# The first layer's feed-forward by seven products of half blocks, on one core

## The chip, the cores and the metric

The kernel runs on one core of a Trainium2 chip. The metric is the device time of one launch in microseconds (us), as the median of some runs. Its engines have queues of their own and work side by side: TensorE (PE) multiplies matrices, VectorE (DVE) and ScalarE (ACT) work on tiles of 128 partitions, GpSimd (POOL) does little here and SyncE (SP) issues most of the transfers. An engine takes its instructions in the order in which they stand in its queue.

## What is computed

Three layers run over 512 positions of 1,024 features in float32. The first layer is a feed-forward, a mixer and a second feed-forward; the change touches the two feed-forwards alone.

```python
D_MODEL, D_FF, SEQ = 1024, 2816, 512

def swiglu(x, w_gate, w_up, w_down):
    return (jax.nn.silu(x @ w_gate) * (x @ w_up)) @ w_down

x = x + 0.5 * swiglu(rms_norm(x, norm_ffn1), ffn1_gate, ffn1_up, ffn1_down)
x = x + mixer(x)
x = x + 0.5 * swiglu(rms_norm(x, norm_ffn2), ffn2_gate, ffn2_up, ffn2_down)
```

## The kernel before

Activations lie with features on the partitions: a tile is 128 features by 512 positions. A float32 product is made of three matmuls. Each operand is split into a high part and a rest (`split`: a cast on ACT, then a subtraction on DVE), and PE adds hi x hi, hi x lo and lo x hi. So a block of 128 output features over 8 input tiles is 24 matmuls of 512 columns into one PSUM bank.

`dense` runs one such block. For it `weights` loads the block's weights (`raw`, 512 KB, on SP's queue), casts them on ACT (`whi`) and subtracts on DVE (`wlo`), from pools of two buffers; `banks` gives the number of PSUM banks for each use (d for blocks, m for small things).

`ffn_swiglu` goes through the 22 tiles of hidden features in parts of 8, 8 and 6 (`FF_TILES`). For each tile it runs a gate block and an up block; DVE multiplies each by r, ACT takes the silu, DVE multiplies both, and `split` makes the hidden tile's two parts. Behind each part come the eight down blocks, each over the part's tiles, and DVE adds half of the block to x. The features enter the first products multiplied by their gain only; r, the reciprocal root of the mean square, is a factor of each position, and is applied behind the product. Its sum of squares (`sum_sq`, on ACT and DVE) and `rstd` (a sum over partitions by matmuls with ones, small steps, two matmuls that spread the result over the partitions, a copy) are written behind the first two blocks. A scheduler puts each engine's instructions in order by priorities, which `sooner` raises (`lead` is 50 here), so that the order in the program need not be that of the code.

The mixer and the other two layers stand in the same order in both kernels.

Of the kernel before, what the change touches and what calls it, by code (L numbers as in the profile page):

```python
# [263 lines left out]
class Model:  # L264
# [336 lines left out]
    def ffn_swiglu(self, f, g):  # L601
        nc, d = self.nc, self.d
        self.lead = 50
        with ExitStack() as es:
            es.enter_context(self.banks(d=4, m=4))
            hp = self.pool(es, f + "h", 2)
            act = self.pair(self.ap, NKT, "x")
            for k in range(NKT):
                self.norm_split(act, g, k)
            j0, r = 0, None  # L610
            for part, n in enumerate(FF_TILES):
                hh = hp.tile([P, 8, S], F32R, tag="hh", name="hh")
# [1655 lines left out]
```

## Time and profile before

| | us |
|---|---|
| median of three runs | 2797.9 (2794.69 to 2798.13) |
| the profiled execution | 2792.82, span 2790.8 |
| PE, DVE, ACT busy in it | 2737.6, 1674.2, 1156.4 |
| first feed-forward | 8.40 to 372.80 |
| second feed-forward | 732.50 to 1096.10 |

The profile is one execution; its span leaves out what lies around the program, 2 us. Busy time is the sum of an engine's instructions, where matmuls overlap and are counted once.

### The profile page before, as it was taken

Reading aid. Unit: us, or ns where it says so; the run is one execution under the profiler, and the core shown is the slowest. Engines: PE = TensorE matmul, PEld = TensorE weight load, DVE = VectorE, ACT = ScalarE, POOL = GpSimd, SP = SyncE. Lnnn points to the kernel's source line nnn. Section 1 sums busy time; section 2 is a strip of 40 time slices with the busy share of each in tenths; the row PEclk is TensorE's granted clock in tenths of the full one; section 3 lists DMA queues with packets and bytes.
Section 4 is the critical chain, followed back from the end, with each engine's and each line's share of the span. In section 5 each row is a group of like instructions: output and inputs, shape, how many; then the busy total and the mean of one; then the engine's idle time right before and its main releaser. Section 6 shows DMA issues by size and latency. Waiting matters only on the chain. (4 is left out here: it accounts for less than half of the span.)

```text
span 2790.8 us, 36154 instructions
## 1 busy us (share of the span) xinstructions
PE 2737.6 (98%) x14502; PEld 2224.3 (80%) x14502; DVE 1674.2 (60%) x2699; ACT 1156.4 (41%) x1758; POOL 79.5 (3%) x165
## 2 busy tenths in 40 slices
PE   8999999999999999999999999999999999999998
PEld 6888877767788888787888888888887878888887
DVE  5444476776643447686345885546846985466456
ACT  4222354553422224565233434444457544343334
POOL 0000000000000000000000011110000000000000
PEclk9999999999999999999999999999999999999999
DMA  4333231110233333322342344443224442312232
GB/s 140 98 99 94 91 131 42 46 51 28 77 97 98 98 96 128 114 83 78 95 138 94 108 164 142 138 133 110 84 76 140 148 148 102 120 69 83 69 105 76
DMA packets 83864, 281.16 MB, mean 101 GB/s; under 512 B 10097, under 2 KB 10609, under 8 KB 82929
## 3 DMA queue, kind: packets, MB, share of 16 engines
q1 hardware_dynamic: 76464, 255.28, 28.2%
q0 software_dynamic: 5888, 18.09, 1.9%
q10 hardware_dynamic: 1344, 5.49, 0.6%
q8 instruction: 113, 1.85, 0.3%
q14 instruction: 55, 0.44, 0.0%
HBM read 254.44 MB, written 23.07 MB: 99 GB/s over the span
## 5 line engine op out<-in xcount | busy, mean ns | idle before, releaser
L366 ACT CAST whi<-raw 128x1024 fp32r<-128x1024 f32 (+4 forms) x454 | 450.5, 993 | 1207.8 <-PE ps_d L391 809.9
L390 PE MATMUL ps_d<-xhi,whi 128*128 128x512 f32 x1896 | 752.2, 397 | 13.9 <-ACT whi L366 9.3
L392 PE MATMUL ps_d<-xhi,wlo 128*128 128x512 f32 x1896 | 743.0, 392 | 3.5 <-DVE wlo L367 3.4
L391 PE MATMUL ps_d<-xlo,whi 128*128 128x512 f32 x1896 | 743.0, 392 | 0.0
L367 DVE TENSOR_TENSOR wlo<-raw,whi 128x1024 fp32r<-128x1024 f32 (+4 forms) x454 | 521.2, 1148 | 156.1 <-ACT whi L366 154.6
L390 PEld LDWEIGHTS ps_d<-xhi,whi 128*128 128x128 f32 x1896 | 357.0, 188 | 94.5 <-ACT whi L366 10.2
L392 PEld LDWEIGHTS ps_d<-xhi,wlo 128*128 128x128 f32 x1896 | 356.9, 188 | 80.9 <-DVE wlo L367 5.3
L391 PEld LDWEIGHTS ps_d<-xlo,whi 128*128 128x128 f32 x1896 | 357.1, 188 | 77.6 <-issue 5.0
L390 PE MATMUL ps_d<-hh,whi 128*128 128x512 f32 x608 | 237.2, 391 | 0.4 <-ACT hh L404 0.4
L392 PE MATMUL ps_d<-hh,wlo 128*128 128x512 f32 x608 | 236.8, 390 | 0.5 <-DVE wlo L367 0.5
L391 PE MATMUL ps_d<-hl,whi 128*128 128x512 f32 x608 | 237.0, 390 | 0.2 <-DVE hl L405 0.2
L390 PEld LDWEIGHTS ps_d<-hh,whi 128*128 128x128 f32 x608 | 114.1, 188 | 25.1 <-ACT hh L404 0.8
L392 PEld LDWEIGHTS ps_d<-hh,wlo 128*128 128x128 f32 x608 | 114.1, 188 | 24.9 <-DVE wlo L367 1.4
L391 PEld LDWEIGHTS ps_d<-hl,whi 128*128 128x128 f32 x608 | 114.1, 188 | 24.4 <-DVE hl L405 1.1
L625 DVE TENSOR_TENSOR hb<-ps_d,rstd 128x512 f32<-128x512 f32 x44 | 30.4, 691 | 135.9 <-PE ps_d L392 135.9
L632 DVE SCALAR_TENSOR_TENSOR x<-ps_d,x 128x512 f32<-128x512 f32 x48 | 33.2, 691 | 116.3 <-PE ps_d L392 116.2
L390 PE MATMUL ps_d<-mixhi,whi 128*128 128x512 f32 x224 | 88.8, 396 | 0.7 <-DVE x L1681 0.6
L624 DVE TENSOR_TENSOR ha<-ps_d,rstd 128x512 f32<-128x512 f32 x44 | 30.4, 691 | 95.8 <-PE ps_d L392 93.2
L392 PE MATMUL ps_d<-mixhi,wlo 128*128 128x512 f32 x224 | 87.7, 392 | 0.0
L391 PE MATMUL ps_d<-mixlo,whi 128*128 128x512 f32 x224 | 87.5, 391 | 0.0
L469 DVE TENSOR_TENSOR acc<-acc,sq 128x512 f32<-128x512 f32 x67 | 46.0, 686 | 25.7 <-ACT sq L468 25.1
L1480 DVE TENSOR_TENSOR x<-ps_d,x 128x512 f32<-128x512 f32 x32 | 22.0, 688 | 61.3 <-PE ps_d L392 61.3
(691 smaller groups left out, 4071.8 us busy)
## 6 DMA issues: line engine op xcount, KB each, us to landing
raw<-in_ffn_gu_dram SPq DMA_DIRECT2D x88, 512.0 KB, 3.5
raw<-in_w_in_dram SPq DMA_DIRECT2D x64, 512.0 KB, 3.5
raw<-in_ffn_dn_dram SPq DMA_DIRECT2D x32, 512.0 KB, 3.5
raw<-in_w_up_dram SPq DMA_DIRECT2D x32, 512.0 KB, 3.5
raw<-in_w_down_dram SPq DMA_DIRECT2D x32, 512.0 KB, 3.9
raw<-in_ret_in_dram SPq DMA_DIRECT2D x32, 512.0 KB, 3.2
raw<-in_ab_in_dram SPq DMA_DIRECT2D x28, 512.0 KB, 3.2
raw<-in_ret_v_dram SPq DMA_DIRECT2D x16, 512.0 KB, 3.2
```

Source lines behind the costliest of these rows:

```text
L366: nc.scalar.copy(hi[:, :n], raw[:, :n])
L367: nc.vector.tensor_sub(lo[:, :n], raw[:, :n], hi[:, :n].bitcast(F32))
L390: PE.matmul(ps, lhsT=hi[:, w], rhs=ah, start=first, stop=False)
L391: PE.matmul(ps, lhsT=hi[:, w], rhs=al, start=False, stop=False)
L392: PE.matmul(ps, lhsT=lo[:, w], rhs=ah, start=False, stop=last)
L469: nc.vector.tensor_add(acc, acc, sq)
L624: nc.vector.tensor_mul(a, pg, r)
L625: nc.vector.tensor_mul(b, pu, r)
L632: nc.vector.scalar_tensor_tensor(out=xm, in0=po, scalar=0.5, in1=xm, op0=ALU.mult, op1=ALU.add)
L1480: nc.vector.tensor_add(xm, po, xm)
```

## The change

In both feed-forwards of the first layer only the first 4 of the 22 tiles of hidden features keep plain blocks of 512 columns (8 blocks). The remaining 18, as gate and up 36 blocks, are taken in nine "fours": a four is a 2x2 matrix of blocks, output features by halves, input features by halves and positions by halves of 256, and is made with seven products in place of eight. The same is done with the down blocks, eight fours over 6, 6, 6 and 4 hidden tiles (`FF_FOURS`). The seven products need sums and differences of the input halves (`inputs` for x, `hidden_parts` for the hidden tiles) and of the weights (`Seven.weights`, where one sum is made by a DMA of GpSimd's queue that adds to what is there), each split like every operand, and their results are added from PSUM by `evac`. A product of an up four has 2 x 4 x 3 = 24 matmuls of 256 columns, so an up four has 168, a down four over six tiles 126, and one over four tiles 84.

PSUM is divided anew: two banks for plain blocks, two for small things, two for x, one for y and one for z of a four. Every third product takes its weight buffers from a third pair. PE's order within a four is b11, t1, t2, b21, t3, then b11 of the next four, then b22 and t4. The inputs of the fours contain r, so they are made behind it: `inputs` is written between the first two blocks and their evacuation.

```diff
-FF_TILES = [8, 8, 6]
+
+FF_FOURS = [3, 3, 3, 2]
...
-            es.enter_context(self.banks(d=4, m=4))
-            hp = self.pool(es, f + "h", 2)
-            act = self.pair(self.ap, NKT, "x")
+            es.enter_context(self.banks(d=2, m=2, x=2, y=1, z=1))
+            sv = Seven(self, self.pool(es, f + "h", 1))
+
+            early = sv.hidden(0)
+            act = tuple(Tiles8(early[8 * k:8 * k + 8]) for k in range(2))
             for k in range(NKT):
                 self.norm_split(act, g, k)
...
-                    pg = self.dense([(d[f + "_gu"][2 * (j0 + j)], 0, NKT)], act)
-                    pu = self.dense([(d[f + "_gu"][2 * (j0 + j) + 1], 0, NKT)], act)
-                    if r is None:
-                        acc = self.sp.tile([P, S], F32, tag="acc", name="acc", bufs=1)
-                        for k in range(NKT):
-                            self.sum_sq(acc, self.x[:, k, :], k)
-                        r = self.rstd(acc, 1e-5)
-                    a = hp.tile([P, S], F32, tag="a", name="ha", bufs=3)
-                    b = hp.tile([P, S], F32, tag="b", name="hb", bufs=3)
-                    nc.vector.tensor_mul(a, pg, r)
-                    nc.vector.tensor_mul(b, pu, r)
-                    nc.scalar.activation(a, a, AF.Silu)
-                    nc.vector.tensor_mul(b, a, b)
-                    self.split(b, hh[:, j, :], hl[:, j, :])
...
+            r, hs = None, {}
+            for j in range(4):
+                pg = self.dense([(d[f + "_gu0"][2 * j], 0, NKT)], act)
+                pu = self.dense([(d[f + "_gu0"][2 * j + 1], 0, NKT)], act)
+                if r is None:
+                    acc = self.sp.tile([P, S], F32, tag="acc", name="acc", bufs=1)
+                    for k in range(NKT):
+                        self.sum_sq(acc, self.x[:, k, :], k)
+                    r = self.rstd(acc, 1e-5)
+                    with self.sooner(-60):
+                        xc = sv.inputs(self.x, lambda k: self.col(g, k), r)
+                if j % 2 == 0:
+                    hs[j // 2] = sv.h()
+                b = sv.mu()
+                h = hs[j // 2][:, j % 2].rearrange("p a t -> p (a t)")
+                nc.vector.tensor_mul(h, pg, r)
+                nc.vector.tensor_mul(b, pu, r)
+                nc.scalar.activation(h, h, AF.Silu)
+                nc.vector.tensor_mul(h, h, b)
...
+            seq = []
+            late = []
+            seq += [(up, (q,), [q] if q < 3 else []) for q in range(2, 4)]
+            seq += [(dn, (0, 0), []), (dn, (0, 1), [3])]
+            seq += [(up, (q,), [q] if q < 6 else []) for q in range(4, 7)]
+            seq += [(dn, (1, 0), []), (dn, (1, 1), [6])]
+            seq += [(up, (q,), [q] if q < 9 else []) for q in range(7, 11)]
+            seq[-1] = (up, (10,), [9, 10])
+            seq += [(dn, (2, 0), []), (dn, (2, 1), []), (dn, (3, 0), []), (dn, (3, 1), [])]
...
+            for fn, args, after in seq:
+                gen = fn(*args) if fn is up else fn(*args, hc[args[0]])
+                next(gen)
+                if last is not None:
+                    next(last[0], None)
+                    for q in last[1]:
+                        halves(q)
+                next(gen)
+                last = gen, after
+            next(last[0], None)
...
+    def inputs(self, x, gain, r):
+
+        nc, f = self.nc, self.f
+        out = dict(zip(self.NAMES, self.inputs_tiles()))
+
+        def normed(t, i, j):
+            for k in range(4):
+                ts = slice(256 * j, 256 * j + 256)
+                nc.vector.scalar_tensor_tensor(out=t[:, k], in0=x[:, 4 * i + k, ts], scalar=gain(4 * i + k),
+                                               in1=r[:, ts], op0=ALU.mult, op1=ALU.mult)
+        ta, tb = (self.h().rearrange("p a b t -> p (a b) t") for _ in range(2))
+        tc, td = (self.raw().rearrange("p (k t) -> p k t", k=4) for _ in range(2))
+        normed(ta, 0, 0)
+        self.split(ta, out["b11"])
+        normed(tb, 0, 1)
+        nc.vector.tensor_sub(ta, tb, ta)
+        self.split(ta, out["t1"])
+        normed(tc, 1, 1)
+        nc.vector.tensor_sub(ta, ta, tc)
+        self.split(ta, out["t2"])
+        normed(td, 1, 0)
...
+    def hidden_parts(self, hc, k, h):
+
+        nc = self.nc
+        at = lambda a: tuple(x[:, k] for x in hc[a])
+        t = self.f.tile([P, 2, 256], F32, tag="ht", name="ht", bufs=1)
+        b11, b12, b21, b22 = h[:, 0, 0], h[:, 0, 1], h[:, 1, 0], h[:, 1, 1]
+        self.split(b11, at("b11"))
+        nc.vector.tensor_sub(t[:, 0], b12, b11)
+        self.split(t[:, 0], at("t1"))
...
+    def weights(self, w):
+
+        nc, m = self.nc, self.m
+        a11, s1, s3 = self.raw(w[0]), self.raw(w[2]), self.raw(w[2])
+        nc.gpsimd.dma_start(out=s1, in_=w[3], accum_op=ALU.add)
+        a12, a22 = m.raw(w[1])[:, :w.shape[2]], m.raw(w[3])[:, :w.shape[2]]
+        yield a11
+        nc.vector.tensor_sub(s3, a11, s3)
+        yield s1
+        nc.vector.tensor_sub(s1, a11, s1)
+        yield s1
+        nc.vector.tensor_add(s1, s1, a12)
+        yield a12
+        yield s3
+        yield s1
+        yield a22
...
+        def product(out, b, first):
+            nonlocal a
+            self.n += 1
+            pool, t = (m.wp, "") if self.n % 3 else (self.f, "3")
+            hi, lo = (pool.tile([P, NKT * P], F32R, tag=x + t, name=x, bufs=1 if t else WB) for x in ("whi", "wlo"))
+            with m.sooner(m.lead):
+                c = a.shape[1]
+                self.split(a, (hi[:, :c], lo[:, :c]))
+                a = next(gen, None)
+            bh, bl = xc[b]
+            for p in range(2):
+                o = out[:, 256 * p:256 * p + 256]
+                for k in range(n):
+                    ws = slice((p * n + k) * P, (p * n + k) * P + P)
+                    for i, (wt, bt) in enumerate(((hi, bh), (hi, bl), (lo, bh))):
+                        mm(o, lhsT=wt[:, ws], rhs=bt[:, k], start=first and p == k == i == 0,
+                           stop=(p == 1 and k == n - 1 and i == 2), skip_group_check=True)
...
+        x = bank["x"]
+        product(x, "b11", True)
+        evac("m1", x)
+        yield
+        y = m.bank("y")
+        product(y, "t1", True)
+        product(x, "t2", False)
+        evac("u2", x)
+        z = m.bank("z")
+        product(z, "b21", True)
+        evac("m2", z)
+        product(x, "t3", False)
+        evac("u3", x)
+        evac("m5", y)
+        yield
+        product(y, "b22", False)
+        evac("y", y)
+        product(x, "t4", False)
+        evac("c21", x)
...
+        def evac(what, ps):
+            ps = four(ps)
+            if what in ("m1", "u2", "u3"):
+                kept[what] = four(self.mu())
+                nc.scalar.copy(kept[what], ps)
+            elif what == "m2":
+                nc.vector.tensor_add(g[:, :, 0], kept["m1"], ps)
+            elif what == "m5":
+                nc.vector.tensor_add(kept["u3"], kept["u3"], ps)
+            elif what == "y":
+                nc.vector.tensor_add(g[:, :, 1], kept["u2"], ps)
+                nc.scalar.activation(g, g, AF.Silu)
+            else:
+                nc.vector.tensor_mul(g[:, :, 0], g[:, :, 0], ps)
+                nc.vector.tensor_mul(g[:, :, 1], g[:, :, 1], kept["u3"])
+                made(g)
...
+            to = {"m1": t(0, 0), "m2": t(0, 0), "u2": t(0, 1), "y": t(0, 1), "c21": t(1, 0), "u3": t(1, 1), "m5": t(1, 1)}[what]
+            nc.vector.scalar_tensor_tensor(out=to, in0=ps.rearrange("p (a t) -> p a t", a=2), scalar=0.5, in1=to,
+                                           op0=ALU.mult, op1=ALU.add)
```

Two places of the new order are shown beside the old, and a third that has no counterpart. The number behind a name is that of the buffer. The first is PE's queue at the start of the first feed-forward: ps_d_161 is block 2, ps_d_248 block 3, L479 the sum over partitions, L494 the spreading of r. Before, the queue around the sum:

```order
L392 MATMUL ps_d_161<-xhi_112,wlo_163 128x512
L390 MATMUL ps_d_248<-xhi_112,whi_249 128x512
L391 MATMUL ps_d_248<-xlo_113,whi_249 128x512
L392 MATMUL ps_d_248<-xhi_112,wlo_250 128x512
L479 MATMUL ps_m_216<-ones_90,acc_190 128x1 x4
L390 MATMUL ps_d_248<-xhi_112,whi_249 128x512
```

and around the spreading:

```order
L390 MATMUL ps_d_248<-xhi_112,whi_249 128x512
L391 MATMUL ps_d_248<-xlo_113,whi_249 128x512
L494 MATMUL ps_m_231<-dg_232,ones_90 128x512
L392 MATMUL ps_d_248<-xhi_112,wlo_250 128x512
L494 MATMUL ps_m_231<-dg_235,ones_90 128x512
L390 MATMUL ps_d_248<-xhi_112,whi_249 128x512
```

Of the changed kernel the same place, where ps_d_169 is block 2, ps_d_300 block 3, L505 the sum and L520 the spreading:

```order
L417 MATMUL ps_d_169<-c13_123,whi_170 128x512
L418 MATMUL ps_d_169<-x2l_115,wlo_171 128x512
L505 MATMUL ps_m_224<-ones_90,acc_198 128x1 x4
L520 MATMUL ps_m_239<-dg_240,ones_90 128x512
L520 MATMUL ps_m_239<-dg_243,ones_90 128x512
L416 MATMUL ps_d_300<-x1h_112,whi_301 128x512
L417 MATMUL ps_d_300<-c6_116,whi_301 128x512
```

Between the sum and the end of the spreading there were matmuls of block 3; now there are none, and block 3 stands behind.

The second is DVE's queue behind r. Before, ps_d_132, 161, 248 and 279 are blocks 1 to 4, and wlo_320 is the rest of block 5's weights:

```order
L624 TENSOR_TENSOR ha_240<-ps_d_132,rstd_238 128x512
L625 TENSOR_TENSOR hb_241<-ps_d_161,rstd_238 128x512
L624 TENSOR_TENSOR ha_310<-ps_d_248,rstd_238 128x512
L367 TENSOR_TENSOR wlo_320<-raw_321,whi_319 128x1024
L627 TENSOR_TENSOR hb_241<-ha_240,hb_241 128x512
L405 TENSOR_TENSOR hl_131<-hb_241,hh_130 128x512
L625 TENSOR_TENSOR hb_311<-ps_d_279,rstd_238 128x512
L627 TENSOR_TENSOR hb_311<-ha_310,hb_311 128x512
```

Now the evacuation of block 3 (ps_d_300) stands behind the building of the inputs (L1333 to L1360) and behind wlo_400, the rest of block 6's weights:

```order
L1353 TENSOR_TENSOR h_256<-h_256,raw2_258 128x1024
L393 TENSOR_TENSOR wlo_400<-raw_401,whi_399 128x1024
L1343 SCALAR_TENSOR_TENSOR raw2_259<-x_79,vec_81,rstd_246 128x256
L1333 TENSOR_TENSOR xlo_249<-h_256,xhi_248 128x1024
L1343 SCALAR_TENSOR_TENSOR raw2_259<-x_79,vec_81,rstd_246 128x256 x2
L1357 TENSOR_TENSOR h_257<-raw2_258,h_257 128x1024
L1360 TENSOR_TENSOR h_256<-h_256,raw2_259 128x1024
L1333 TENSOR_TENSOR xlo_249<-raw2_259,xhi_248 128x1024
L1333 TENSOR_TENSOR x0l_251<-h_257,x0h_250 128x1024
L654 TENSOR_TENSOR h_294<-ps_d_300,rstd_246 128x512
```

The evacuations of blocks 1 and 2 stand further ahead, directly behind r.

The third is DVE's queue in an up four in the middle of the first feed-forward. L1468 to L1472 evacuate b21's, t3's and b22's results; wlo_1870 belongs to b22, wlo_1900 to t4, and those from 1950 on to the next four (L1400 makes a weight sum for it):

```order
L1468 TENSOR_TENSOR h_1580<-mu_1622,ps_z_1764 128x2x256
L1333 TENSOR_TENSOR wlo_1870<-raw2_1583,whi_1869 128x1024
L1333 TENSOR_TENSOR wlo_1900<-raw_1590,whi_1899 128x1024
L1470 TENSOR_TENSOR mu_1822<-mu_1822,ps_y_1703 128x512
L1333 TENSOR_TENSOR wlo_1950<-raw2_1828,whi_1949 128x1024
L1400 TENSOR_TENSOR raw2_1828<-raw2_1826,raw2_1828 128x1024
L1472 TENSOR_TENSOR h_1580<-mu_1762,ps_y_1703 128x2x256
L1333 TENSOR_TENSOR wlo_1979<-raw2_1828,whi_1978 128x1024
```

Each evacuation of the second bank (ps_y) stands behind the splits of weights for products that come later on PE.

## Rows read from the trace of the kernel before

**Rows 1.** The page's line on busy time: engine, us, share of the span, instructions. PEld is the loading of weights.

```profile
PE 2737.6 (98%) x14502; PEld 2224.3 (80%) x14502; DVE 1674.2 (60%) x2699; ACT 1156.4 (41%) x1758; POOL 79.5 (3%) x165
```

**Rows 2.** Busy time in stretches: from:to, length, then busy us and instructions of PE, PEld, DVE, ACT and POOL, the granted clock of PE, the DMA engines' share, GB/s. The first ends the first feed-forward behind its eight first blocks; the others are the whole feed-forwards.

```profile
57.10:372.80 315.70, 315.70 (x1393) 261.20 (x1393) 144.04 (x171) 91.57 (x112) 0.19 (x1) 1.00 0.30 96
...
8.40:372.80 364.40, 363.41 (x1595) 299.40 (x1596) 174.90 (x216) 114.59 (x144) 2.13 (x2) 1.00 0.32 101
732.50:1096.10 363.60, 362.70 (x1595) 299.51 (x1596) 174.92 (x220) 110.19 (x137) 1.14 (x3) 1.00 0.30 95
```

**Rows 3.** Timeline (start, length, engine, line, operation, and in brackets idle time before it and its releaser) around r and the ends of blocks 4 and 8 in the first feed-forward, and around r and the end of block 4 in the second.

```profile
22.28 1.05 PE L479 MATMUL ps_m<-ones,acc 128*128 128x1 f32 x8 [0.18 <-DVE acc L469]
...
28.00 0.51 PE L494 MATMUL ps_m<-dg,ones 128*128 128x512 f32 x1
...
28.55 0.59 ACT L496 COPY rstd<-ps_m 128x512 f32<-128x512 f32 x1 [6.27 <-PE ps_m L494]
...
29.17 0.69 DVE L624 TENSOR_TENSOR ha<-ps_d,rstd 128x512 f32<-128x512 f32 x1 [1.22 <-ACT rstd L496]
...
35.37 0.69 DVE L625 TENSOR_TENSOR hb<-ps_d,rstd 128x512 f32<-128x512 f32 x1 [0.57 <-PE ps_d L392]
...
57.13 0.69 DVE L625 TENSOR_TENSOR hb<-ps_d,rstd 128x512 f32<-128x512 f32 x1 [3.31 <-PE ps_d L392]
...
752.00 0.69 DVE L624 TENSOR_TENSOR ha<-ps_d,rstd 128x512 f32<-128x512 f32 x1 [1.36 <-ACT rstd L496]
...
758.64 0.69 DVE L625 TENSOR_TENSOR hb<-ps_d,rstd 128x512 f32<-128x512 f32 x1 [1.94 <-PE ps_d L392]
```

**Rows 4.** Timeline of PE in the third layer's mixer: the first of six matmuls of 512 columns in a row, the first behind them, the first of six of 256 and the first behind them, all on weights loaded for them; and, elsewhere, the first of three of 256 and the first behind them.

```profile
2441.85 0.39 PE L2145 MATMUL ps_m<-qh,kh 128*128 128x512 f32 x1
...
2443.21 0.33 PE L2145 MATMUL ps_m<-qh,kh 128*128 128x384 f32 x1
...
2444.27 0.28 PE L2145 MATMUL ps_m<-qh,kh 128*128 128x256 f32 x1
...
2444.98 0.22 PE L2145 MATMUL ps_m<-qh,kh 128*128 128x128 f32 x1
...
2453.45 0.29 PE L2158 MATMUL ps_m<-sch,vhi 128*128 128x256 f32 x1
...
2453.82 0.22 PE L2158 MATMUL ps_m<-sch,vhi 128*128 128x128 f32 x1
```

**Rows 5.** DVE's groups by line and shape: operation, out<-in, count, busy us and mean ns of one, idle time before them.

```profile
L367 DVE TENSOR_TENSOR wlo<-raw,whi 128x1024 fp32r<-128x1024 f32 x374 | 456.9, 1222 | 155.3 <-ACT whi L366 154.6 <-issue 0.3
...
L632 DVE SCALAR_TENSOR_TENSOR x<-ps_d,x 128x512 f32<-128x512 f32 x48 | 33.2, 691 | 116.3 <-PE ps_d L392 116.2
...
L625 DVE TENSOR_TENSOR hb<-ps_d,rstd 128x512 f32<-128x512 f32 x44 | 30.4, 691 | 135.9 <-PE ps_d L392 135.9
...
L458 DVE SCALAR_TENSOR_TENSOR xlo<-x,vec,xhi 128x512 fp32r<-128x512 f32 x40 | 28.8, 745 | 2.4 <-ACT xhi L457 2.4
L367 DVE TENSOR_TENSOR wlo<-raw,whi 128x512 fp32r<-128x512 f32 x40 | 27.2, 683 | 0.5 <-PE ps_d L392 0.5
...
L367 DVE TENSOR_TENSOR wlo<-raw,whi 128x768 fp32r<-128x768 f32 x16 | 15.3, 958 | 0.0
...
L1883 DVE TENSOR_TENSOR mt<-bb,pw 128x256 f32<-128x256 f32 x32 | 12.4, 418 | 0.1
```

**Rows 6.** Timeline of DVE: the last two evacuations of the first feed-forward, and three operations in a row that wait for nothing, later.

```profile
368.73 0.69 DVE L632 SCALAR_TENSOR_TENSOR x<-ps_d,x 128x512 f32<-128x512 f32 x1 [1.17 <-PE ps_d L392]
...
372.81 0.69 DVE L632 SCALAR_TENSOR_TENSOR x<-ps_d,x 128x512 f32<-128x512 f32 x1 [0.69 <-PE ps_d L392]
...
1194.31 1.22 DVE L367 TENSOR_TENSOR wlo<-raw,whi 128x1024 fp32r<-128x1024 f32 x1
1195.45 0.69 DVE L1394 TENSOR_TENSOR ig<-ig,th 128x512 f32<-128x512 f32 x1
1196.05 0.75 DVE L1340 SCALAR_TENSOR_TENSOR mx<-ps_t,vec,bs 128x512 f32<-128x512 f32 x1
```

**Rows 7.** ACT's groups of weight casts, columns as in rows 5.

```profile
L366 ACT CAST whi<-raw 128x1024 fp32r<-128x1024 f32 x374 | 393.1, 1051 | 1022.9 <-PE ps_d L391 657.0 <-issue 252.4 <-PE ps_t L580 48.7
...
L366 ACT CAST whi<-raw 128x768 fp32r<-128x768 f32 x16 | 13.4, 838 | 35.4 <-PE ps_d L391 22.4 <-issue 13.1
```

**Rows 8.** Stretches as in rows 2, behind the first feed-forward, where PE waits for 2.32 us.

```profile
385.00:387.00 2.00, 0.06 (x1) 0.00 (x0) 1.50 (x2) 1.98 (x3) 0.00 (x0) 1.00 0.77 315
...
388.00:390.00 2.00, 2.00 (x6) 1.61 (x5) 1.44 (x2) 1.97 (x4) 0.10 (x1) 0.50 0.62 244
```

**Rows 9.** Timeline of PE there: the first matmul behind the wait, and the eighth.

```profile
387.38 0.79 PE L390 MATMUL ps_d<-xhi,whi 128*128 128x512 f32 x1 [2.32 <-DVE pb L726]
...
390.53 0.49 PE L391 MATMUL ps_d<-xlo,whi 128*128 128x512 f32 x1
```

**Rows 10.** The page's DMA queue of POOL (packets, MB, share of 16 engines) and its line of the gate/up loads on SP's queue (count, KB each, median us from issue to landing).

```profile
q0 software_dynamic: 5888, 18.09, 1.9%
...
raw<-in_ffn_gu_dram SPq DMA_DIRECT2D x88, 512.0 KB, 3.5
```

More of the change, by code (lines that the diff above doesn't have):

```diff
@@ L87, with quarters, gate_up_first @@
 Q_PERM = np.concatenate([np.concatenate([np.arange(64) + 64 * i, np.arange(64) + 64 * (4 + i)]) for i in range(4)])
+def quarters(w, n, cols):
+    w = w.reshape(2, n, P, -1, P)
+    out = np.empty((cols.shape[0], 2, 2, P, 2, n, P), np.float32)
+    for q in range(cols.shape[0]):
+        for p in range(2):
+            for i in range(2):
+                out[q, i, :, :, p] = w[:, :, :, cols[q, p, i]].transpose(0, 2, 1, 3)
+    return out.reshape(cols.shape[0], 4, P, 2 * n * P)
+def gate_up_first(g, u):
+    return np.concatenate([col_blocks(g[:, :4 * P])[:, None], col_blocks(u[:, :4 * P])[:, None]], 1).reshape(-1, P, NKT * P)
 def gate_up(g, u):
-    return np.concatenate([col_blocks(g)[:, None], col_blocks(u)[:, None]], 1).reshape(-1, P, NKT * P)
+    w = np.concatenate([g, u], 1)
+    q = np.arange(2, 11)[:, None, None]
+    p, i = np.arange(2)[None, :, None], np.arange(2)[None, None, :]
+    return quarters(w, 4, 22 * i + 2 * q + p)
 def down(w):
     out, f = [], 0
-    for n in FF_TILES:
-        out.append(col_blocks(w[f:f + n * P]))
-        f += n * P
+    q, p, i = np.arange(2)[:, None, None], np.arange(2)[None, :, None], np.arange(2)[None, None, :]
+    for n in FF_FOURS:
+        part = w[f * 2 * P:(f + n) * 2 * P].reshape(n, 2, P, 1024).transpose(1, 0, 2, 3).reshape(2 * n * P, 1024)
+        out.append(quarters(part, n, 4 * q + 2 * p + i))
+        f += n
     return out
@@ L211, in layout @@
     for f in ("ffn1", "ffn2"):
+        a[f + "_gu0"] = gate_up_first(i[f + "_gate"][0], i[f + "_up"][0])
         a[f + "_gu"] = gate_up(i[f + "_gate"][0], i[f + "_up"][0])
@@ L319, in setup @@
             if k in (0, 3):
-                self.early.append(self.raw(self.d["ffn1_gu"][k // 3]))
+                self.early.append(self.raw(self.d["ffn1_gu0"][k // 3]))
         nc.sync.dma_start(out=self.cst, in_=self.d["cst"])
@@ L604, in ffn_swiglu @@
         with ExitStack() as es:
-            es.enter_context(self.banks(d=4, m=4))
-            hp = self.pool(es, f + "h", 2)
-            act = self.pair(self.ap, NKT, "x")
+            es.enter_context(self.banks(d=2, m=2, x=2, y=1, z=1))
+            sv = Seven(self, self.pool(es, f + "h", 1))
+            early = sv.hidden(0)
+            act = tuple(Tiles8(early[8 * k:8 * k + 8]) for k in range(2))
             for k in range(NKT):
                 self.norm_split(act, g, k)
-            j0, r = 0, None
@@ new lines, in up, with made, dn, halves @@
+            def up(q):
+                def made(h):
+                    hs[q] = h
+                return sv.four(d[f + "_gu"][q - 2], 4, xc, sv.swiglu(made))
+            def dn(c, m, hc):
+                return sv.four(d[f"{f}_dn{c}"][m], FF_FOURS[c], hc, sv.residual(self.x, m))
+            hc = [None] * 4
+            group = lambda c: range(sum(FF_FOURS[:c]), sum(FF_FOURS[:c + 1]))
+            def halves(q):
+                c = next(c for c in range(4) if q in group(c))
+                if hc[c] is None:
+                    hc[c] = sv.halves(c, FF_FOURS[c])
+                sv.hidden_parts(hc[c], q - group(c)[0], hs.pop(q))
@@ L636, in first_block @@
+            halves(0)
+            halves(1)
+            last = None
+            for fn, args, after in seq:
[8 more added lines that the diff above has]
+            next(last[0], None)
     def first_block(self):
```

91 lines of the change are left out of this document (81 added, 10 removed).

## The prediction

> **What bounds the kernel now.** I read the page's engine lines first: TensorE (PE) is busy for 98% of the span, VectorE (DVE) for 60%, ScalarE (ACT) for 41% [rows 1]. A share over the whole span says nothing of one stage, so I cut out the two feed-forwards that change. The first runs from 8.40 to 372.80 us, the second from 732.50 to 1096.10. In both PE works nearly without a hole, 363.41 of 364.40 and 362.70 of 363.60 us, and DVE only 175 [rows 2]. After the first eight gate/up blocks the first one holds 315.70 us that are full to the last digit: 1,392 matmuls of 512 columns, 0.2268 each. So fewer PE microseconds are worth what they cost, if DVE, whose work the change doubles, keeps out of the way.
>
> The third view is the timeline at the start, where the norm's factor r is made [rows 3]. The token sums run at 22.28, the second of two spreading matmuls at 28.00, r is copied by ACT at 28.55, and DVE multiplies the first block by it at 29.17. What the reader is to see: block 4 ends at 35.37 and block 8 at 57.13, which is 5.44 per block; PE filled the time until r with blocks 3 and 4. In the second feed-forward r comes at 752.00, block 4 ends at 758.64.
>
> **A, the matmuls.** Behind the plain blocks, 1,392 of 512 columns go and 9x168 + 6x126 + 2x84 = 2,436 of 256 come. Six starts of 512 columns run from 2441.85 to 2443.21, 0.2268 each; six of 256 from 2444.27 to 2444.98, 0.1183 each; three elsewhere 0.123 [rows 4]. Each loads weights of its own (PE and PEld have 14,502 each [rows 1]), so the loads are in the number. 2,436 x 0.1183 = 288.2 against 315.7: **-27.5** per feed-forward. Bounds: exactly half of 0.2268 gives -39.5, 0.123 gives -16. I take the six in a row, the case most like a product.
>
> **B, the gap before r.** The plain blocks now have two banks instead of four. In the new order (shown with the change), token sums and both spreads stand right behind block 2, and block 3 waits for a bank that DVE frees by its first multiplication with r. Behind block 3 the whole program of PE waits. That multiplication runs 0.69 from about 29.17 [rows 3], so block 3 starts near 29.95 and block 4 ends at 29.95 + 10.88 = 40.83, against 35.37: 5.5 late. In the second feed-forward 752.85 + 10.88 = 763.7 against 758.64: 5.1. A pause has a second price: after 2.32 us without work at 385 the granted clock stood at 0.50 for some three microseconds [rows 8], and seven matmuls took from 387.38 to 390.53, 3.15 instead of 7 x 0.2268 = 1.59 [rows 9]: 1.6 more. **+7.1**, and +6.7 in the second.
>
> **C, the gap before block 5.** DVE's order after r holds the building of the seven inputs between the two evacuations. Block 5 waits for the bank of block 3, which the multiplication h<-ps_d_300 frees; ahead of it in DVE's queue stands wlo_400, the weights of block 6, and these need the cast into block 4's buffer, so the end of block 4. From there: cast 1.05 [rows 7], split 1.14, then three scaled copies of 256 (an estimate of 0.40 each: 0.75 for 512, less the 0.27 between 512 and 256 columns of a two-tensor operation, less an overlap of 0.08 [rows 5]), five operations of 1024 at 1.14 from start to start [rows 6], then 0.69 + 0.05 until PE. 1.05 + 1.14 + 1.2 + 5.7 + 0.74 = 9.8 with nothing for PE to do, and 1.6 of clock: **+11.4**. Bounds: 8.5 without a fallen clock and with the casts of the inputs early, 12 with full durations.
>
> **D, the change from plain to seven.** From the end of block 8 to the split of the fourth product's weights (wlo_661), DVE's order holds 2 operations of 512, 5 of 1024 and 11 of 256. The 256 takes 0.42 [rows 5], 0.34 from start to start by the same overlap of 0.08 that 1024 shows (1.22 against 1.14 [rows 5, 6]). 1.3 + 5.7 + 3.7 + 0.3 of hand-over = 11.0; PE's three products ahead last 3 x 24 x 0.1183 = 8.5. **+2.5.** Below, nothing, if the 11 narrow ones fit in earlier holes.
>
> **E, DVE in the steady part.** For an up four DVE has 7 splits and 3 weight sums of 1024, 5 evacuations of 512, 11 narrow ones for hidden parts. From start to start 10x1.14 + 5x0.60 + 11x0.34 = 18.1 us, by full durations 20.3 [rows 5, 6]; PE 168 x 0.1183 = 19.9. A down of three: 10x0.87 + 7x0.61 = 13.0 (14.4 by durations) against 14.9. Of two: 10x0.60 + 7x0.61 = 10.3 (11.7) against 9.9. All fours: 262 or 292 us against PE's 288. So DVE goes from 48% to over 90%, and what matters is single waits:
> - In each up the evacuation of m5 (mu<-ps_y, 0.69) stands behind the split of t4's weights, and the product b22 behind it. That split waits for t3's buffer: t3's end, which comes 0.16 after the next start (0.28 against 0.118 [rows 4]), then cast 1.05, begun 0.12 before the end since the buffer's last use is a matmul earlier, split 1.14, m5 0.69, hand-overs 0.15: 3.1 against one product of 2.84. 0.3 in each of nine: 2.7.
> - Downs of three have shorter products (2.1): cast 0.84, split 0.87, evacuation 0.69 and hand-overs give 2.5, 0.4 late where a down follows and less where an up does, an estimate of 0.35: 2.1 in six.
> - The last four downs also hold the hidden parts of two h at once: 2x13.0 + 22x0.34 + 2x10.3 = 54.0 against 49.7, 4.3, and with 1.4 for the shortest products' hand-overs 5.7.
> Together **+10.5.** Bounds: 0 (everything slips into holes) and, with full durations and a hand-over of 0.05 on some 25 rows of each of 17 fours, 292 - 288 + 21 = 25. I take the chain's value, near the middle.
>
> **F.** At the end x came piece by piece, one evacuation every 4.08 us (368.73, 372.81 [rows 6]); now three evacuations of the last four fall behind its last products where one did, two more starts at 0.61: **+1**.
>
> Costed at nothing: ACT, 13 of 20 us in an up, hidden by PE (0.5 each if it slips). Loads: six of 512 KB for a four instead of four in as long, issued 20 to 30 us ahead by the pools, where one takes 3.5 [rows 10]; PE's work covers them. The accumulating DMA is in no trace; from below it costs a plain load, from above I leave it for a rival.
>
> **Sum.** First: -27.5 + 7.1 + 11.4 + 2.5 + 10.5 + 1.0 = +5.0; second +4.6; together +9.6. The profiled execution took 2792.8 and would take 2802.4. The median of the runs is 2797.9, 5.1 above it, so I give **2807.5**. A change under 0.2% (5.6 us) can't be told from none.
>
> **Rivals.**
> 1. Faster: DVE keeps ahead of PE, D, E and F are nothing. For it: 262 of 288 us; against it: the m5 chain. -9.0 and -9.4, so **2779.5**. It decides where D+E+F falls under 6.4 per feed-forward (14.0 in my sum).
> 2. No measurable change: D+E+F between 6.4 and 12.0, **2798**.
> 3. DVE is the bound throughout: E at 25, **2836**. For it the full durations, 292; against it the start-to-start rows.
> 4. Half the columns at exactly half the time, 0.1134: 12.0 less per feed-forward, **2783.5**. Against it the nine starts of 256 columns, none closer than 0.118. The Trainium skill ("TensorE: Matmul & The Clock Gate", "Wait — 56ns, not 53.3ns?") gives columns over 2.4 GHz and 2.5 ns, an estimate of 109 ns here, by which the time would be some 2763 (22 less in each); its 215.7 for 512 columns isn't what the rows show either (226.8).
> 5. The accumulating DMA takes more than its lead of some 20 us. q0's present traffic is 18 MB [rows 10], which shows no such transfer. At 3 us beyond it per four, 34 x 3 = 100: **2907**.
>
> **How the numbers follow.** My forecast, slower by 0.2 to 1%: 0.39. Rival 1: 0.28. Rival 2: 0.20. Rival 3: 0.07. Rival 4: 0.04. Rival 5: 0.02. With rivals 1 and 4 faster, 3, 5 and the forecast slower: faster 0.32, same 0.20, slower 0.48. The range 2775 to 2835 reaches over rivals 1, 2 and 4 and to rival 3; the forecast's own is 2803 to 2826.
>
> **What would show it.** In the changed profile: 256-column matmuls start 0.118 apart inside a product (A); PE idle some 7 us behind the second spread, released by DVE mu L655 (B), and 10 us ahead of block 5, released by h L654 (C), each followed by some three us at clock 0.5; block 8 ends near 75 instead of 57.1; PE waits of 0.3 on DVE L1470 in each up; DVE about 0.9 busy in the seven-product part. The prediction is wrong if the starts stand closer, if one of the gaps is filled, or if waits in the steady part sum to under 7 or over 20 us per feed-forward.

## The result, and the profile after

The changed kernel takes 2825.4 us (2824.9 to 2826.8, four runs), the one before beside it 2798.0 (2794.7 to 2798.9): a ratio of 1.0102, interval 1.0086 to 1.0118. Slower, as forecast, and inside the range of 2775 to 2835, but by 27 us where the forecast said 9.6. The profiled execution has a span of 2823.1 against 2790.8. That is 32.3, since the one shown of before lay 5 us under its median and this one at its median; the account below is of the 32.3.

The page's line on busy time answers to [rows 1]:

```profile
PE 2717.9 (96%) x16590; PEld 2299.4 (81%) x16590; DVE 1988.6 (70%) x3217; ACT 1311.1 (46%) x2036; POOL 109.7 (4%) x199
```

PE works 20 us less, DVE 314 more, and the span is longer, so PE waits more. Stretches as in [rows 2], the first feed-forward's plain blocks and fours and the second's:

```profile
8.29:77.50 69.21, 53.06 (x202) 41.75 (x203) 51.83 (x80) 30.83 (x44) 3.01 (x2) 0.88 0.37 127
77.50:382.60 305.10, 298.10 (x2437) 293.80 (x2436) 273.47 (x386) 157.75 (x234) 15.72 (x19) 1.00 0.50 142
...
752.78:821.40 68.62, 52.52 (x203) 41.79 (x204) 47.93 (x76) 27.13 (x38) 1.93 (x2) 0.85 0.29 93
821.40:1127.00 305.60, 297.78 (x2437) 293.74 (x2436) 272.88 (x386) 156.79 (x232) 14.33 (x18) 1.00 0.49 142
```

The fours take 305.1 where the blocks took 315.7, so the seven products do pay, 10.6 us. The eight plain blocks ahead of them take 69.2 where they took 48.7. Read from one place to the next, as the start of the same matmul in both traces, after minus before:

| place | first | second |
|---|---|---|
| first matmul | -0.1 | 20.3 |
| end of block 2 | 0.8 | 21.5 |
| end of block 4 (gap B lies between) | 8.4 | 28.8 |
| end of block 8 (gap C) | 20.6 | 41.2 |
| last matmul of the fours | 10.1 | 31.2 |
| 400 matmuls into the next stage | 20.9 | 35.2 |

At the end of the program 32.5 are left. The two gaps stand in PE's timeline, with what released them:

```profile
23.09 1.05 PE L505 MATMUL ps_m<-ones,acc 128*128 128x1 f32 x8 [0.87 <-DVE acc L495]
28.21 1.39 PE L520 MATMUL ps_m<-dg,ones 128*128 128x512 f32 x2 [4.08 <-DVE dg L518]
31.01 0.79 PE L416 MATMUL ps_d<-x1h,whi 128*128 128x512 f32 x1 [1.40 <-DVE mu L655]
...
53.47 0.76 PE L416 MATMUL ps_d<-x1h,whi 128*128 128x512 f32 x1 [9.77 <-DVE h L654]
```

Block 3 waits for L655, the first multiplication with r, and block 5 for L654 behind the building of the inputs, 9.77 us, as foreseen. Of gap B's idle time 0.87 and 4.08 us lie ahead of the sums and the spreading of r, and only 1.40 behind them, where the prediction looked for some 7. The clock around the second gap (columns as in [rows 2]; the number behind POOL's is the granted clock, 0.50 its lower level):

```profile
48.00:53.40 5.40, 0.00 (x0) 0.00 (x0) 5.40 (x7) 2.13 (x3) 0.90 (x1) 0.50 0.81 187
53.40:58.00 4.60, 4.53 (x11) 3.59 (x12) 4.52 (x10) 1.40 (x3) 0.00 (x0) 0.50 0.20 75
58.00:60.00 2.00, 2.00 (x10) 1.67 (x9) 0.35 (x2) 0.00 (x0) 0.00 (x0) 0.97 0.00 0
```

It had fallen by 48.00, some four microseconds after block 4's last matmul ended (43.70), and stood at 0.50 for another 4.6 us when PE had work again: 2.3 lost, where 1.6 was taken from a shorter pause [rows 8, 9]. Next the step of term A. From the first of these two starts to the second there are 24 matmuls of 256 columns, one product:

```profile
77.51 0.28 PE L1433 MATMUL ps_x<-xhi,whi 128*128 128x256 f32 x1
...
80.39 0.28 PE L1433 MATMUL ps_y<-xhi,whi 128*128 128x256 f32 x1
```

That is 0.120 each, and so it is for 2,381 of the 2,436 in one feed-forward (mean 0.1199). Behind the first feed-forward, PE's timeline and then DVE's:

```profile
384.89 0.40 PE L417 MATMUL ps_d<-xlo,whi 128*128 128x512 f32 x1
390.51 0.79 PE L418 MATMUL ps_d<-xhi,wlo 128*128 128x512 f32 x1 [5.23 <-DVE wlo L393]
```

```profile
387.38 0.68 DVE L495 TENSOR_TENSOR acc<-acc,sq 128x512 f32<-128x512 f32 x1
387.98 0.74 DVE L484 SCALAR_TENSOR_TENSOR xlo<-x,vec,xhi 128x512 fp32r<-128x512 f32 x1
388.64 0.68 DVE L495 TENSOR_TENSOR acc<-acc,sq 128x512 f32<-128x512 f32 x1
389.25 1.22 DVE L393 TENSOR_TENSOR wlo<-raw,whi 128x1024 fp32r<-128x1024 f32 x1
```

PE stands 5.23 us with the high products done and waits for the rest of the weights (wlo L393). It stands in DVE's queue behind the splits of x (L484) and the squares' sums (L495) of pieces that came last. Finally the adding DMA, on the page:

```profile
q0 software_dynamic: 10784, 33.30, 5.1%
...
raw<-in_ffn_gu_dram POOLq DMA_DIRECT2D x18, 512.0 KB, 6.2
```

It lands in 6.2 us where a plain load takes 3.3. In the trace each of the 34 has landed 6.5 us or more before ACT begins to cast its sum, so nothing waits for it here.

### The profile page after: what moved, and what is told of

Read it like the earlier page. It is cut to its first block, busy times and chain, and to the rows that moved or that the text cites. A ratio compares the mean times of both kernels' runs of the same rounds, so it can differ in the third digit from the quotient of the medians.

```text
span 2823.1 us, 41519 instructions
## 1 busy us (share of the span) xinstructions
PE 2717.9 (96%) x16590; PEld 2299.4 (81%) x16590; DVE 1988.6 (70%) x3217; ACT 1311.1 (46%) x2036; POOL 109.7 (4%) x199
## 5 line engine op out<-in xcount | busy, mean ns | idle before, releaser
L392 ACT CAST whi<-raw 128x1024 fp32r<-128x1024 f32 (+2 forms) x334 | 327.5, 981 | 781.3 <-PE ps_d L417 539.7
L416 PE MATMUL ps_d<-xhi,whi 128*128 128x512 f32 x1192 | 478.0, 401 | 4.5 <-DVE pb L789 2.3
L418 PE MATMUL ps_d<-xhi,wlo 128*128 128x512 f32 x1192 | 470.3, 395 | 9.1 <-DVE wlo L393 9.0
L393 DVE TENSOR_TENSOR wlo<-raw,whi 128x1024 fp32r<-128x1024 f32 (+2 forms) x334 | 378.7, 1135 | 137.5 <-ACT whi L392 136.2
L417 PE MATMUL ps_d<-xlo,whi 128*128 128x512 f32 x1192 | 469.4, 394 | 0.5 <-DVE xlo L554 0.5
L1332 ACT CAST whi<-raw 128x1024 fp32r<-128x1024 f32 (+2 forms) x238 | 219.5, 923 | 281.0 <-PE ps_x L1433 113.4
L1333 DVE TENSOR_TENSOR wlo<-raw,whi 128x1024 fp32r<-128x1024 f32 (+2 forms) x238 | 252.3, 1064 | 41.2 <-ACT whi L1332 39.1
L416 PEld LDWEIGHTS ps_d<-xhi,whi 128*128 128x128 f32 x1192 | 225.1, 189 | 58.1 <-issue 7.6
L417 PEld LDWEIGHTS ps_d<-xlo,whi 128*128 128x128 f32 x1192 | 224.9, 189 | 50.7 <-issue 5.2
L416 PE MATMUL ps_d<-hh,whi 128*128 128x512 f32 x256 | 100.6, 393 | 0.4 <-ACT hh L430 0.4
L417 PE MATMUL ps_d<-hl,whi 128*128 128x512 f32 x256 | 99.8, 390 | 0.2 <-DVE hl L431 0.2
L418 PE MATMUL ps_d<-hh,wlo 128*128 128x512 f32 x256 | 99.7, 389 | 0.0
```

The costliest lines, as they stand in the source:

```text
L392: nc.scalar.copy(hi[:, :n], raw[:, :n])
L393: nc.vector.tensor_sub(lo[:, :n], raw[:, :n], hi[:, :n].bitcast(F32))
L416: PE.matmul(ps, lhsT=hi[:, w], rhs=ah, start=first, stop=False)
L417: PE.matmul(ps, lhsT=hi[:, w], rhs=al, start=False, stop=False)
L418: PE.matmul(ps, lhsT=lo[:, w], rhs=ah, start=False, stop=last)
L1332: self.nc.scalar.copy(pair[0], src)
```

## Experiments

All are edits of the changed kernel and have its work, unless said. They ran in other batches, so they are compared by their ratio to the kernel before in the same batch; the changed kernel's is 1.0102, and 0.001 is 2.8 us. Lines of the form "PE a <- DVE b" are PE's waits: what waited, for what, then us in total, times, and the longest.

**Inputs later.**

```diff
-                    with self.sooner(-60):
+                    with self.sooner(-300):
```

> The building of the seven inputs gets a lower priority (300 behind instead of 60), nothing else. Theory of separate prices: the gap before block 5 (9.8 us idle and some 2.4 of slow clock in each feed-forward) is only the order of DVE's queue, so it goes: 2825 - 24 = 2801. Rival, DVE's throughput: from r to the first down fours DVE has more work than PE, the 19 us of the inputs only move and PE waits for them later, so that only the slow clock is saved: 2817 to 2825.

Ratio 1.0015 (1.0005 to 1.0024), 24 us less than the changed kernel. The whole stretch from r to the fours, and the border of blocks 4 and 5:

```profile
29.00:64.50 35.50, 34.85 (x144) 28.69 (x145) 33.33 (x52) 17.71 (x24) 1.07 (x1) 0.92 0.38 119
...
42.61 0.39 PE L418 MATMUL ps_d<-x2l,wlo 128*128 128x512 f32 x1
42.84 0.39 PE L416 MATMUL ps_d<-x1h,whi 128*128 128x512 f32 x1
```

Block 5 follows in 0.23. DVE has the same work in 35.5 us, 94% busy, instead of 48.5. The theory of separate prices holds here, 24 us as it said: gap C was the order of a queue, and its work fitted under four blocks of PE.

**Banks of y and z for plain blocks.**

```diff
-                pg = self.dense([(d[f + "_gu0"][2 * j], 0, NKT)], act)
-                pu = self.dense([(d[f + "_gu0"][2 * j + 1], 0, NKT)], act)
+                pg = self.dense([(d[f + "_gu0"][2 * j], 0, NKT)], act, "dy"[j % 2])
+                pu = self.dense([(d[f + "_gu0"][2 * j + 1], 0, NKT)], act, "dz"[j % 2])
```

> Blocks 3 and 4, 7 and 8 take the banks that y and z will have later, so four plain blocks can stand before r. Theory of separate prices: the gap before r (8.3 us with its clock in each feed-forward) goes, 2825 - 16 = 2809. Rival, DVE's throughput: r and DVE's work behind it are where they were, so the gap before block 5 only becomes longer by as much: 2820 to 2826.

Ratio 1.0017 (1.0008 to 1.0026), 24 us less, more than either theory said. Gap B is gone (block 4 ends 0.2 later than before, instead of 8.4), and of gap C this is left in the first feed-forward:

```profile
PE ps_y L416 <- DVE h L654: 5.1, 1, 5.1
```

The bank that waits for the inputs to be built is now y's, which is wanted again by block 7 and not by block 5 (nor is it block 5 that waits, as the next expectation has it): two more blocks cover DVE's work. So this edit took part of gap C too, and doesn't give B's price.

**Both.**

> Both edits at the start together: y's and z's banks for blocks 3, 4, 7 and 8, and the inputs at the lower priority. In the run with the banks alone PE still waited 5.2 us ahead of block 5 with some 2 us of slow clock behind, twice. Theory of separate prices: these go too, 2799.6 - 14.5 = 2785, below the kernel before. Rival, DVE's throughput: blocks 3 to 8 now end some 8 us earlier than with the inputs alone, DVE can't have the inputs and the first weights by then, and the waits at the first four grow by 3 to 7 us in each: 2791 to 2799.

Ratio 1.0013 (1.0004 to 1.0022): no more than one alone. From r to the end of the plain blocks, then the first fours, and PE's longest waits in them:

```profile
27.00:57.60 30.60, 29.86 (x131) 24.22 (x130) 28.82 (x51) 16.50 (x23) 0.00 (x0) 1.00 0.36 132
57.60:100.00 42.40, 33.54 (x248) 32.09 (x247) 36.16 (x49) 20.82 (x32) 2.80 (x3) 0.92 0.48 123
...
PE ps_y L1433 <- ACT whi L1332: 2.9, 1, 2.9
...
PE ps_y L1433 <- DVE mu L1470: 1.8, 1, 1.8
PE ps_z L1433 <- ACT whi L1332: 1.5, 1, 1.5
```

Now the fours begin at 57.7 with no gap ahead of them, and block 8 ends 0.7 later than in the kernel before. But PE idles 8.9 of the next 42.4 us: gap B's 8 us are lost again, and the time, 2799.4, lies just above the rival's range. DVE was busy for 28.8 of the 30.6 us ahead and isn't through with the inputs, as the rival says. Yet the longest of these waits, 2.9, doesn't end with DVE's work: ACT waited for a load, here and at the second four.

```profile
63.59 1.04 ACT L1332 CAST whi<-raw 128x1024 fp32r<-128x1024 f32 x1 [4.63 <-DMA raw<-in_ffn_gu_dram]
...
88.32 1.05 ACT L1332 CAST whi<-raw 128x1024 fp32r<-128x1024 f32 x1 [5.95 <-DMA raw<-in_ffn_gu_dram]
```

Both casts begin 0.1 after the adding DMA has landed (63.49 and 88.22); in the changed kernel 22.9 and 12.1 us lie between. The first was issued at 57.90, once the load that it adds to had landed at 57.59. That load was issued at 51.4, close behind one that had waited in SP's queue until DVE's split of a plain block's weights (wlo L393) freed its buffer at 50.5. So banks and priorities alone don't give B's 8 us. That DVE's throughput is what takes them is not shown: DVE's late work and the chain of load, adding DMA and cast both stand here, and no run has both edits with these loads issued earlier or without the adding DMA.

**The order at the mixer's start.**

```diff
-    def norm_in(self, g):
+    def norm_in(self, g, late=0):
...
-            self.sum_sq(acc, self.x[:, k, :], k)
+            with self.sooner(-late):
+                self.sum_sq(acc, self.x[:, k, :], k)
...
-            act, acc = self.norm_in("norm_mix")
+            act, acc = self.norm_in("norm_mix", 60)
...
+            self.lead = 60
             x.first = [self.dense([(d["w_in"][12], 0, NKT)], act)]
+            self.lead = 0
```

> In the changed kernel, only the start of the mixer is reordered: the weights of its first two blocks stand ahead of the last splits of x, and the sums of squares behind them. Theory: PE's wait of 5.2 us for the rest of the first block's weights, with some 2.4 us of slow clock behind it, is only the order of DVE's queue at the hand-over: 2825 - 7.6 = 2818. Rival: the eight pieces of x are late in any order, the wait goes to the splits of x: 2822 to 2826.

Ratio 1.0088 (1.0073 to 1.0103), some 4 us less, with intervals that overlap. PE's waits from 300 to 420 us:

```profile
PE ps_d L418 <- DVE wlo L393: 3.8, 2, 3.4
PE ps_m L521 <- DVE dg L519: 2.0, 1, 2.0
```

The 5.2 is gone but for 0.4. The 3.4 is not new: it is a wait for a later block's weights, which the kernel before has too, from 380 to 440 us:

```profile
PE ps_d L392 <- DVE wlo L367: 3.4, 1, 3.4
```

In the changed kernel it stands at 424, and here it comes earlier. New are 2.0, and 0.6 ahead of it, for the mixer's own r, whose sums now come later. The loss behind the first feed-forward falls from 10.8 to 5.9, by 4.9 us of the theory's 7.6; behind the second feed-forward another layer follows, which this edit doesn't touch. Of "its first two blocks" the edit raises the weights of the first alone.

**Both downs of the first half of x ahead.**

```diff
-            seq += [(dn, (2, 0), []), (dn, (2, 1), []), (dn, (3, 0), []), (dn, (3, 1), [])]
+            seq += [(dn, (2, 0), []), (dn, (3, 0), []), (dn, (2, 1), []), (dn, (3, 1), [])]
```

> The last four downs in another order: both that complete the first half of x, then both of the second half. Theory: the hand-over to the next stage (10.8 us lost behind the first feed-forward, 4.0 behind the second) comes from eight pieces of x that DVE must split and square all at once; with four of them ready some 25 us earlier it falls by about half to two thirds, 2814 to 2818. Rival: the hidden parts of the last two tiles are then needed one down earlier and DVE is late for them by as much: 2822 to 2828.

Ratio 1.0104 (1.0089 to 1.0119), no difference. In the trace the loss behind the first feed-forward falls from 10.8 to 5.6, but its last matmul is 1.9 later; behind the second it falls by 1.4, and the feed-forward is 1.6 longer. Both were right in kind, and what is left can't be told from nothing.

**All three: banks, inputs, mixer.** 

> Banks, inputs and the order at the mixer's start together. If the three prices are separate: 2785 - 7.6 = 2777, 0.6% below the kernel before. If DVE is the bound at the start of the fours: 2785 to 2791, no difference that matters.

Ratio 1.0005 (0.9997 to 1.0014), 2795.5 us, above both ranges: the losses of the run with banks and inputs stay.

**Inputs and mixer.** 

> The two edits that came out well apart from each other, the inputs at the lower priority (2825.4 to 2798.7) and the mixer's start (2825.4 to 2819.7); banks as in the changed kernel. They lie at the two ends of the feed-forward and don't compete for the same stretch of DVE, so their prices should add: 2793, 0.1% below the kernel before. Rival: the mixer's start gives nothing where it begins earlier, 2797 to 2799.

Ratio 1.0001 (0.9992 to 1.0010), the sum of the two ratios' gains. In time it is 2796.3, between the 2793 that was expected, from absolute times of different batches, and the rival's 2797; the interval overlaps that of the inputs alone. Both stand level with the kernel before; no version beat it.

**Two pairs of weight buffers.**

```diff
-            pool, t = (m.wp, "") if self.n % 3 else (self.f, "3")
+            pool, t = m.wp, ""
```

> The changed kernel without the third pair of weight buffers: all products take turns with two. Each split of weights can then only begin when the product two before has ended and must be ready within one product. Cast 1.05, begun 0.12 early, and split 1.22 with hand-overs take about 2.3 of 2.84 us in an up, 1.9 of 2.13 in a down of three; with other work in DVE's queue each comes late by 0.3 to 1: 119 products in each feed-forward, 2825 + 70 to 2825 + 240. If DVE's order keeps them in time, 2825 to 2835.

Ratio 1.0273 (1.0258 to 1.0289), 48 us more. Of PE's waits these grew most (from 1.4 and 1.8 in the changed kernel), by 23 us:

```profile
PE ps_z L1433 <- DVE wlo L1333: 15.1, 14, 1.3
PE ps_x L1433 <- DVE wlo L1333: 10.9, 25, 0.8
```

Single waits are small, and the whole lies under the lower end of what was expected; the third pair is worth 0.2 us per product (48 over 2 x 119).

**The sum by DVE instead of the adding DMA.**

```diff
-        nc.gpsimd.dma_start(out=s1, in_=w[3], accum_op=ALU.add)
...
+        nc.vector.tensor_add(s1, s1, a22)
         nc.vector.tensor_sub(s3, a11, s3)
```

> The changed kernel without the adding DMA: the sum of two weight blocks is one more addition of full width on DVE for each four, and one load less. By throughput: DVE 19.3 of 19.9 us in an up, 13.9 of 14.9 in a down of three; if the m5 chain and single waits are what counts, little changes: 2825 to 2835. If DVE's throughput is the bound, 17 x 1.14 in each feed-forward: 2825 + 39 = 2864. If the adding DMA itself held something up (it lands in 6.2 us where a plain load takes 3.3), the time falls below 2825.

Ratio 1.0121 (1.0107 to 1.0135), some 5 us more, with intervals that overlap. The middle of the first feed-forward, the changed kernel and then this one:

```profile
100.00:320.00 220.00, 219.13 (x1807) 217.38 (x1806) 195.18 (x265) 114.53 (x165) 9.50 (x11) 1.00 0.53 152
```

```profile
100.00:320.00 220.00, 218.80 (x1810) 217.46 (x1810) 205.18 (x277) 114.64 (x166) 0.00 (x0) 1.00 0.39 127
```

DVE takes on 10 us of these 220 and PE is busy for only 0.3 less. So in this stretch DVE, 89% busy, is not the bound: at 93% PE keeps its pace. What bounds behind r and at the end this run doesn't tell.

**Weight sums on GpSimd.**

```diff
-        nc.vector.tensor_sub(s3, a11, s3)
+        nc.gpsimd.tensor_sub(s3, a11, s3)
...
-        nc.vector.tensor_sub(s1, a11, s1)
+        nc.gpsimd.tensor_sub(s1, a11, s1)
...
-        nc.vector.tensor_add(s1, s1, a12)
+        nc.gpsimd.tensor_add(s1, s1, a12)
```

> The three weight sums of each four are made by GpSimd instead of DVE, 10 instead of 13 operations of full width fewer to more on DVE: 7 splits stay. Theory that DVE's throughput makes the waits inside the fours (13.0 us in each feed-forward by the trace, 3.3 at the first four): DVE has 3.4 us less of 18 in an up, the waits fall to about 5, 2825 - 16 = 2809. Rival, chains (cast, split, evacuation): they stay, 2821 to 2826. If GpSimd takes more than some 6 us for one sum, it becomes the bound and the time rises by tens of us.

Ratio 1.0528 (1.0511 to 1.0546). A sum of 1024 columns took 2.7 to 2.95 us on average, under the 6 that were to be feared, and still the time rose by 119. One GpSimd addition, and DVE's subtractions of 256 columns beside and behind it:

```profile
154.96 2.47 POOL L1398 TENSOR_TENSOR raw<-raw,raw 128x1024 f32<-128x1024 f32 x1 [1.46 <-DMA raw<-in_ffn_gu_dram]
```

```profile
155.10 2.60 DVE L1333 TENSOR_TENSOR c<-ht,c 128x256 fp32r<-128x256 f32 x1
...
159.82 0.42 DVE L1333 TENSOR_TENSOR c<-ht,c 128x256 fp32r<-128x256 f32 x1
```

The one that starts at 155.10 ends 2.60 later, at 157.70, 0.27 after GpSimd; the one at 159.82, alone, takes 0.42. By groups (columns as in [rows 5]), the changed kernel and then this one:

```profile
L1333 DVE TENSOR_TENSOR c<-h,c 128x256 fp32r<-128x256 f32 x54 | 22.6, 419 | 0.0
...
L1472 DVE TENSOR_TENSOR h<-mu,ps_y 128x512 f32<-128x512 f32 x18 | 12.3, 683 | 4.4 <-PE ps_y L1433 4.4
```

```profile
L1333 DVE TENSOR_TENSOR c<-h,c 128x256 fp32r<-128x256 f32 x54 | 47.9, 902 | 0.0
...
L1472 DVE TENSOR_TENSOR h<-mu,ps_y 128x512 f32<-128x512 f32 x18 | 12.4, 687 | 22.3 <-PE ps_y L1433 22.3
```

Subtractions with both inputs in SBUF doubled on average. The evacuations of L1472, which read one input from PSUM, kept their 0.68, though in the trace all 18 overlap a GpSimd addition. The Trainium skill ("SBUF — State Buffer", "Who interferes with whom") says that a DVE instruction with two SBUF inputs contends with a GpSimd instruction that reads SBUF; the trace agrees, with 902 against 419. So DVE gained nothing: it is busy for 1998.0 us against 1988.6, though 102 sums, some 108 us of its work, are gone. How much of the 119 is this, and how much that GpSimd takes 2.7 us and more for a sum where DVE took 1.22, ahead of the same splits, isn't separated.

**The other sums on GpSimd,** those of the inputs and the hidden tiles (their eight `tensor_sub` and `tensor_add` from nc.vector to nc.gpsimd), on the kernel with all three edits, and on the one with inputs and mixer.

> On the kernel with banks, inputs and the mixer's start changed, the four sums of the inputs and the four of each hidden tile go to GpSimd, which was at 2.7 to 2.95 us for 1024 columns, an estimate of 0.8 for 256. They are needed late, unlike the weight sums. DVE has some 4.6 us less at the start and 1.4 less per hidden tile. If DVE's throughput at the start is what PE waits for (some 12 us in each feed-forward with both edits): 2795 - 16 = 2779. Rival: DVE's splits of these sums stand in its queue ahead of weights and wait for GpSimd as with the weight sums: 2800 or more.

> The same sums on GpSimd, with the inputs' priority and the mixer's start changed but the two banks kept. Without the sums on GpSimd this would be 2798.7 - 5.7 = 2793. The gap before r stays, so DVE has 8 us more before the fours: if its throughput counts, waits of 2 to 3 us at the first fours go as well, 2787. Rival as before, DVE waits in order for GpSimd: 2798 or more.

Ratios 1.0078 (1.0063 to 1.0093) and 1.0099 (1.0083 to 1.0116), 20 and 27 us more than without. GpSimd's slowest group of 256 columns, and DVE's, in the first:

```profile
L1374 POOL TENSOR_TENSOR ht<-ht,h 128x256 f32<-128x256 f32 x22 | 28.7, 1303 | 5.7 <-DVE h L658 4.1
```

```profile
L1334 DVE TENSOR_TENSOR c<-h,c 128x256 fp32r<-128x256 f32 x54 | 34.8, 645 | 0.0
```

The four groups of 256 columns average 0.90 to 1.30 us, not the 0.8 estimated, and DVE's neighbours 645 ns instead of 419. What was taken off DVE came back as longer operations: it is busy for 2005.8 us against 1986.4 with the three edits alone. So these two runs don't test DVE's throughput, as they were meant to.

## Why the prediction came out as it did

**B, C.** Right in place, cause and size: 7.6 and 12.2 us against 7.1 and 11.4, in the second 7.3 and 12.4 against 6.7 and 11.4. Most of the difference is the clock, which stood at 0.50 for 4.6 and 5.1 us behind the two gaps C and 4.0 behind the second B, where the sum has 1.6 us lost, some 3.2 at 0.50; in the first B it is block 3, which starts 0.3 later than worked out. Blocks 1 and 2 lost another 1 us each time, which had no term. What the prediction did not say is that B's time is used, by DVE and by the first fours' loads; as prices to be saved the two don't add up.

**D, E.** 305.1 - 2,436 x 0.1199 = 13.0 us of waits in the fours of the first feed-forward, 13.5 in the second; the sum had 13.0. By place 3.3 in the first four, 3.8 in the middle, 5.9 in the last downs, against 2.5, 4.8 and 5.7. Rivals 1, 2 and 3 fell with it. For the middle the closeness is partly luck. The prediction's sign for it, a wait of 0.3 on L1470 in each up, is listed once in the waits of the first feed-forward:

```profile
PE ps_y L1433 <- DVE mu L1470: 0.2, 1, 0.2
```

The 3.8 are mostly some sixteen pauses of 0.1 to 0.7, with 1.3 us of them behind L1470, where the sum had 2.7.

**A was mis-sized.** The term took 0.1183 and got 0.1199, 292.1 instead of 288.2: 3.9 us in each. That lies inside the term's own bounds. All nine starts of 256 columns in [rows 4] take 0.71 + 0.37 = 1.08 us, 0.120 each; the prediction took the six in a row and left the other three as a bound. The six end on a matmul of 128 columns:

```profile
2444.75 0.28 PE L2145 MATMUL ps_m<-ql,kh 128*128 128x256 f32 x1
2444.87 0.28 PE L2145 MATMUL ps_m<-qh,kl 128*128 128x256 f32 x1
```

By these hundredths the last step, from 2444.87 to 2444.98, looks shorter (0.11 after 0.12). It isn't the cause: in the trace's nanoseconds the six steps are 118, 117, 118, 119, 121 and 117, and the five between equal shapes still average 118.6. Why the products' matmuls start 1.3 ns further apart than those five is not shown. Rival 4, faster still, fell with it.

**F was mis-sized most:** +1 in each, measured +10.8 and +4.0. The term counted the evacuations that come late. It left out what the next stage does with them: a split and a square's sum for each piece of x, 0.66 + 0.60 from start to start. Before, they were done under the downs, one piece every 4.08 us; now five splits and four sums stand between the last evacuation and the mixer's first weights, 5 x 0.66 + 4 x 0.60 = 5.7 us. That makes the wait of 5.23, half of the 10.8. Another 1.3 is a wait just ahead of it for a cast, and the clock has most of the rest. It stood at 0.50 behind the 5.23, and again behind the 3.4 us wait that both kernels have, where in the kernel before it stayed full. The changed kernel, then the one before:

```profile
391.00:396.00 5.00, 5.00 (x13) 3.84 (x13) 1.20 (x2) 0.00 (x0) 0.00 (x0) 0.50 0.95 391
424.40:430.00 5.60, 5.60 (x13) 4.04 (x13) 5.60 (x10) 0.72 (x1) 0.00 (x0) 0.50 0.44 140
```

```profile
406.20:412.00 5.80, 5.80 (x24) 4.44 (x25) 5.80 (x10) 0.72 (x1) 0.00 (x0) 1.00 0.45 117
```

These two cost 2.8 and 2.9 us; 1.6 comes off, since the pause of [rows 8, 9] keeps its clock now. Behind the second feed-forward the largest of several waits is 2.2 us for the next r, where it was 0.4.

**Rival 5** fell by the landing time and by the run without the adding DMA. With banks and inputs changed, though, that DMA's landing did end PE's longest wait in the fours.

In the sum A was short by 7.8 us, F by 12.8, B and C by 2.9, and blocks 1 and 2 by 2.1; 2.7 came back in later layers, 0.6 between the two and 0.1 ahead of the first; E took 0.5 more in the second: 22.7 of the 22.9 between 9.6 and 32.5. The forecast's direction stood on the two gaps, which held. A, B, C and F were all off to the same side; only the places within D and E offset each other. The time lies at the upper edge of the forecast's own 2803 to 2826.

## What to carry over

What the fewer multiplications gained here was lost where the preparation of operands piled up: look at how much DVE, ACT and the loads have to do between two points that PE can't pass, not at a busy share over the stage. A result that becomes ready all at once moves its consumer's preparation from cover to the critical path, so cost the next stage's use of it too, and the clock behind each wait. And where rows of the same shape disagree, as 0.118 and 0.123 did, take the step from all of them.

## Of the hardware

Beside GpSimd's additions DVE's operations with two SBUF inputs took longer (419 to 902 ns on average at 256 columns, and 2.60 us for one that lay almost whole under an addition of 2.47), which made GpSimd no free helper here. In the seven products a matmul of 256 columns with its own weights starts every 0.1199 us, 1.06 of half of 0.2268.
